# One slice of attention output work half a step later, function tables loaded in other stages, and a later first store

## The chip, the cores and the metric

The kernel runs on one core of one Trainium2 chip. The time is that of one whole launch, from inputs in the chip's main memory to outputs there, in device microseconds (us). Lower is better. PE is the tensor engine (matmuls; its weight loads overlap them), DVE the vector engine, ACT the scalar engine, POOL the general engine, SP the engine whose queue issues most transfers. Every engine works its own list of instructions in the order in which the program was written, and waits on semaphores for the others.

## The reference

A two-layer encoder trunk on one sequence of 256 tokens, width 1024, float32. Layer 0 mixes tokens by latent attention (MLA), layer 1 by forgetting attention (FoX). Around each mixer stand two half-step feed-forward blocks, and a gated per-layer embedding (PLE) ends the layer.

```python
for i in range(DEPTH):
    h = h + 0.5 * swiglu(rms_norm(h, ffn_norm[i, 0]), ffn_w_in[i, 0], ffn_w_out[i, 0])
    u = rms_norm(h, mix_norm[i])
    if i % N_MIXERS == 0:
        h = h + mla_mixer(u, cos, sin, ...)      # 8 heads, ends in o @ w_o
    else:
        h = h + fox_mixer(u, ...)                # 8 heads, ends in o @ w_o
    h = h + 0.5 * swiglu(rms_norm(h, ffn_norm[i, 1]), ffn_w_in[i, 1], ffn_w_out[i, 1])
    gate = jax.nn.sigmoid(rms_norm(h, ple_norm[i]) @ ple_w_gate[i])
    h = h + gate * (p[i] @ ple_w_proj[i])
return rms_norm(h, final_norm)
```

## The kernel before

The residual `state` stays on the chip, transposed: 8 blocks of 128 features by 256 tokens. All weights stream in once, as a list of 128x1024 tiles (`plan`). Class `Weights` brings each through three steps: SP issues the transfer into `raw`, ACT rounds it to `whi` (L98), DVE subtracts to get the rest, `wlo` (L102). PE then multiplies activations by both parts (L228 with `whi`, 512 columns; L229 with `wlo`, 256 columns). `W.pump()` prepares one tile; `W.catch_up()` does so only when fewer than a given number of tiles are ready ahead of the one in use. Where the calls stand in the program sets where these instructions stand in ACT's and DVE's lists.

The feed-forward stage `ffn` ends in a loop over 8 output blocks `d`: PE fills `po`, DVE adds it to `state` (L384), ACT and DVE write the next stage's input `u` and its square.

Both mixers end in `attention`. Its loop over `h` (a "step" below) is a pipeline of heads. In step h, DVE scales the probabilities of head h-2 (`shares`, tile `pr`), PE transposes those of head h-lag (`turn`, tile `pt`, copied to `ptS` by ACT), PE makes the scores of head h-1 (`scores`, tile `psc`; then maximum on DVE, `nm`, exponential on ACT at L425 and L426), and PE multiplies by the values of head h-lag (`values`, tile `po`), which ACT (L208) and DVE (L209) split into `os`. The lag is 3 in MLA, 2 in FoX. In MLA's steps 0 to 5 PE also projects queries; from step 6 on it has only this chain and the output projection w_o.

`fill_some(n)` hands PE n pairs of w_o matmuls (L228, L229), each pair one head of one output block (tile `ps`, named `ps2` in the source), taking only heads below `ready`. A step has two places for it: place 0 before `turn`, place 1 behind `scores` and ahead of `values`. `MLA_FILLS` and `FOX_FILLS` say how many at (step, place).

`ple_by_token` ends the kernel: per half of the tokens (t) and per column half or quarter, PE computes a gate, `gated` runs sigmoid (ACT L810), multiply and add (DVE L811, L812), square with a sum (ACT L813) and a gain multiply (DVE L814). `store(t)` turns the sums into a factor (DVE L820, L821, POOL L822), scales two halves (ACT L823, DVE L824) and issues two output transfers (L826).

ACT needs the right function table before an exponential, sigmoid, sine, logarithm or silu; the compiler puts an ACT_TABLE_LOAD ahead of the first that needs another one. `ready[P, 1]` with `AF.Silu` at L190 loads the first table while inputs are on their way.

Of the kernel before, what the change touches and what calls it, by code (L numbers as in the profile page):

```python
# [11 lines left out]
F32 = mybir.dt.float32  # L12
# [3 lines left out]
AF = mybir.ActivationFunctionType  # L16
ALU = mybir.AluOpType
# [23 lines left out]
GAINS = 80  # L41


MLA_FILLS = {(6, 0): 3, (7, 0): 3, (8, 0): 3, (8, 1): 4, (9, 0): 4, (9, 1): 4, (10, 1): 3}
FOX_FILLS = {(8, 0): 4, (8, 1): 7, (9, 0): 6, (9, 1): 5}

PI_IN = 3.1415925
# [94 lines left out]
def trunk(ctx, tc, xT, xt, pT, pos, freq, bf, ffn_first, ffn_in, ffn_out, w_down, w_uq, w_ukv, mla_o,  # L142
# [42 lines left out]
    state = const.tile([P, GAINS + KD * T], F32, name="state")  # L185
    g_sb, hT = state[:, :GAINS], state[:, GAINS:].rearrange("p (k t) -> p k t", k=KD)

    ready = const.tile([P, 1], F32, name="ready")
    nc.vector.memset(ready, 0.0)
    nc.scalar.activation(ready, ready, AF.Silu)  # L190
    ident = const.tile([P, P], F32, name="ident")
    make_identity(nc, ident)
    ones = const.tile([P, P], F32, name="ones")
# [117 lines left out]
            self.rb2 = self.rb.rearrange("p (o t) -> p o t", o=1).to_broadcast([P, 2, T])  # L311


    def ffn(norm, nxt, first=None, meanwhile=None, later=None):
        hs = big.tile([P, KF, 2, T], F32R, name="hs", tag="big")
        meanwhile = meanwhile or iter(())
        gu, hid = {}, {}

        def evacuate(c, i, ps):
            two = work.tile([P, 2, T], F32, name="two", tag="pair2", bufs=4)  # L320
            nc.vector.tensor_mul(two, ps, norm.rb2)  # L321
            gu[c, i] = tmp("gu")
            nc.gpsimd.tensor_add(gu[c, i], two[:, 0, :], two[:, 1, :])  # L323

        def hidden(c):
            h = hid.pop(c)
            split(hs[:, c, 0, :], hs[:, c, 1, :], h)

        def gate(c, ps, pumps=1):
            evacuate(c, 0, ps)  # L330
            W.pump(pumps)
            if c:
                hidden(c - 1)
            sg = tmp("sg")
            nc.scalar.activation(sg, gu.pop((c, 0)), AF.Silu)  # L335
            gu[c, 0] = sg

        def up(c, ps, pumps=1):
            evacuate(c, 1, ps)
            hid[c] = tmp("hid")  # L340
            nc.gpsimd.tensor_mul(hid[c], gu.pop((c, 0)), gu.pop((c, 1)))  # L341
            W.pump(pumps)
            if c % 2:
                W.catch_up()

        waits = [(bank("pg"), bank("pu"))]
        if first:
            waits.append((bank("pg"), bank("pu")))
            first([p for ps in waits for p in ps])
        else:  # L350
            blocks(waits[0], norm.pair)
            W.pump(2)
        at = len(waits)
        for c in range(at, KF):
            pg = bank("pg")
            block(pg, norm.pair)
            if c == at:
                norm.by_token()
                W.pump()
            else:  # L360
                gate(c, pg)
            pu = bank("pu")
            block(pu, norm.pair)
            if c == at:
                norm.by_column()
                for x, ps in enumerate(waits):
                    gate(x, ps[0], x)
                    up(x, ps[1], 0)
                gate(c, pg)
            up(c, pu, c > at)  # L370
        for d in range(KD):
            ps = bank("po")
            for a in range(0, KF, KD):
                w, = W.get()
                part(ps, w, hs, range(a, min(a + KD, KF)), KF - 1, at=lambda k: (k - a) * P)
                W.done(w)
                if a + KD < KF:
                    W.pump()
                    if d == a == 0:
                        hidden(KF - 1)  # L380
                    for _ in range(2):
                        next(meanwhile, None)
            for i in range(2):
                nc.vector.scalar_tensor_tensor(hT[:, d, :], ps[:, i, :], 0.5, hT[:, d, :], op0=ALU.mult, op1=ALU.add)  # L384
            if d < KD - 1:
                nxt.high(d, hT[:, d, :])
                W.pump()
                nxt.low(d, hT[:, d, :])
                nxt.square(hT[:, d, :])
            else:  # L390
                nxt.last(d, hT[:, d, :])
                W.pump()
            W.catch_up()
            for _ in range(2):
                next(meanwhile, None)
            if later:
                later(d)
        for _ in meanwhile:
            pass


    def attention(project, score, v, scale, nxt, lag, fills, early, cumq=None):
# [92 lines left out]
        for h in range(H + lag):  # L495
            if 0 <= h - 2 < H:
                shares(h - 2)
            if h == H:
                W.pump()
            if h < H and not late:  # L500
                project(h, 0)
            fill_some(fills.get((h, 0), 0))
            if 0 <= h - lag:
                turn(h - lag)
            if h < H and late:
                project(h, 0)
            if 0 <= h - 1 < H:
                scores(h - 1)
            if h < H:
                project(h, 1)  # L510
            W.catch_up()
            fill_some(fills.get((h, 1), 0))
            if 0 <= h - lag:
                values(h - lag)
            if h >= H:
                W.catch_up()
            ready = h - lag + 1
        for n in (H - 1, H):
            for d in range(early):
                fill(d, n)  # L520
# [115 lines left out]
    def fox(norm, nxt):  # L636
# [11 lines left out]
        def gates():  # L648
# [10 lines left out]
            nc.vector.tensor_scalar(u, e, 1.0, None, op0=ALU.add)  # L659
            nc.vector.scalar_tensor_tensor(e, u, 1.0, e, op0=ALU.subtract, op1=ALU.subtract)  # L660
            nc.scalar.activation(u, u, AF.Ln)
            yield
            nc.vector.tensor_sub(u, u, e)
            nc.vector.scalar_tensor_tensor(z, z, 0.0, u, op0=ALU.min, op1=ALU.subtract)
# [89 lines left out]
    def ple(pp, norm, nxt):  # L754
# [20 lines left out]
        for c in range(2):  # L775
            w, = W.get()
            for i in range(4):
                if i % 2 == 0:
                    pe = bank("pe")
                if (c, i) == (1, 3):  # L780
                    norm.by_column()
                part(pe[:, i % 2, :], w, pp, range(2), at=lambda k: k * 512 + i * P)
                if i % 2:
                    nc.scalar.activation(es[:, 4 * c + i - 1:4 * c + i + 1, :], pe, AF.Copy)
            W.done(w)
            if c == 0:
                norm.by_token()
            W.pump(2)
        for d in range(KD):
            ps = bank("ps", (P, T))  # L790
            block(ps, norm.pair)
# [2 lines left out]
    def ple_by_token(pp, norm):  # L794
# [21 lines left out]
        def store(t, n):  # L816
# [3 lines left out]
            nc.vector.reduce_sum(s, sums[:, t, :n], axis=AX.X)  # L820
            nc.vector.tensor_scalar(v, s, 1.0 / D, EPS, op0=ALU.mult, op1=ALU.add)  # L821
            nc.gpsimd.tensor_tensor(r, v, mhalf[:, :1], op=ALU.pow)  # L822
            nc.scalar.activation(h[:, t, half[0]], es[:, t, half[0]], AF.Copy, scale=r)  # L823
            nc.vector.tensor_scalar(h[:, t, half[1]], es[:, t, half[1]], r, None, op0=ALU.mult)  # L824
            for e, a in zip((nc.scalar, nc.sync), half):
                e.dma_start(out[t * P:(t + 1) * P, a], h[:, t, a])  # L826


        for c in range(2):
# [32 lines left out]
        for t in range(2):  # L862

            cuts = [half[1]] if t == 0 else [slice(N, N + N // 2), slice(N + N // 2, D)]
            for i, a in enumerate(cuts):
# [2 lines left out]
                    b = (k % 2 - 1) * N  # L868
                    rows(last, ws[k // 2], norm.pair, k, slice(a.start + b, a.stop + b), t, KD - 1)
                gated(t, last, a, 1 + i)  # L870
            store(t, 1 + len(cuts))
        W.done(*ws)


# [159 lines left out]
                yield  # L1034

    n1 = Norm(G_MIX, KD, D)
    ffn(n0, n1, first, tables())
    for i in range(2):
        n2 = Norm(G_FFN + 8 * (2 * i + 1), KD, D)
        if i == 0:  # L1040
# [2 lines left out]
            fox(n1, n2)  # L1043
        n3 = Norm(G_PLE + 8 * i, KD, D)
        p = Embedding(i)
        ffn(n2, n3, later=p)
        if i == 0:
            n0, n1 = Norm(G_FFN + 16, KD, D), Norm(G_MIX + 8, KD, D)
            ple(p.pair, n3, n0)
            ffn(n0, n1)  # L1050
        else:
            ple_by_token(p.pair, n3)

# [89 lines left out]
```

## Time and profile before

| | |
|---|---|
| time, median of 3 runs | 1018.78 us (1017.39 to 1019.54) |
| time of the profiled execution | 1017.48 us |
| its span, first to last instruction | 1015.4 us |
| PE busy | 993.2 us, 98% |
| DVE busy | 741.9 us, 73% |
| ACT busy | 517.2 us, 51% |
| POOL busy | 424.7 us, 42% |
| granted PE clock, mean | 0.994 of full speed |

The profiled execution took 2.1 us beside its span. A share of busy time is a mean over stages, so the rows further down look at single stages: who is idle, and for whom it waits.

### The profile page before, as it was taken

The page shows a single profiled execution, that of the slowest core. Times are in us where ns is not written, and L with a number is a line of the kernel's source. Part 1 is how long each engine was busy: PE and PEld are TensorE (multiplying, and loading weights), DVE is VectorE, ACT ScalarE, POOL GpSimd, SP SyncE. Part 2 cuts the span into 40 slices and gives each one's busy share as a digit, 9 for nine tenths or more (in the row PEclk, how much of TensorE's full clock was granted, in tenths as well). Part 3 has the DMA queues.
Part 4 walks back from the last instruction along what each step waited for, and adds up shares of the span by engine and source line. Part 5 has one row for each costly group of instructions (what it writes and reads, how often), then busy time and mean ns, then how long its engine had stood idle before and what let it go on. Part 6 is the DMA issues. An engine that isn't in the chain of part 4 may idle for free.

```text
span 1015.4 us, 16002 instructions
## 1 busy us (share of the span) xinstructions
PE 993.2 (98%) x5940; PEld 877.1 (86%) x5940; DVE 741.9 (73%) x1050; ACT 517.2 (51%) x821; POOL 424.7 (42%) x348
## 2 busy tenths in 40 slices
PE   9999999997999999999999999999999999999996
PEld 7888888986888888889888888889888888888885
DVE  5777878674677888667877887666776778876674
ACT  7555544464455545446555544456544555444553
POOL 0777720110157776111377774120221477672110
PEclk9999999998999999999999999999999999999999
DMA  9567666541257656665457666655542566666561
GB/s 325 174 208 209 196 177 194 185 146 45 79 173 210 200 187 177 202 192 187 132 188 210 197 187 178 201 183 170 183 146 85 186 207 194 191 184 205 174 205 42
DMA packets 51388, 180.54 MB, mean 178 GB/s; under 512 B 5872, under 2 KB 6000, under 8 KB 51312
## 3 DMA queue, kind: packets, MB, share of 16 engines
q1 hardware_dynamic: 50736, 178.49, 56.5%
q8 instruction: 47, 0.77, 0.3%
q10 hardware_dynamic: 576, 1.05, 0.3%
q14 instruction: 29, 0.24, 0.1%
HBM read 178.46 MB, written 1.05 MB: 177 GB/s over the span
## 4 chain that ended last, share of the span: by engine, by line
PE 92%; DVE 4%; ACT 2%; issue 1%; DMA 1%; SPq 0%; POOLq 0%; POOL 0%; ACTq 0%
PE po L228 16%; PE pu L228 16%; PE pg L228 16%; PE po L229 8%; PE pu L229 8%; PE pg L229 8%; PE ps L228 5%; PE ps L229 2%; PE ps L215 1%; PE ps L214 1%; PE ps L213 1%; DVE wlo L102 1%; PE pv L213 1%; PE pv L215 1%; PE pv L214 1%
## 5 line engine op out<-in xcount | busy, mean ns | idle before, releaser
L102 DVE TENSOR_TENSOR wlo<-raw,whi 128x1024 fp32r<-128x1024 f32 (+2 forms) x338 | 418.2, 1246 | 10.6 <-ACT whi L98 10.0
L98 ACT ACTIVATE whi<-raw 128x1024 fp32r<-128x1024 f32 (+2 forms) x338 | 335.9, 1027 | 21.7 <-DMA raw<-in_ffn_in_dram 12.5
L323 POOL TENSOR_TENSOR gu<-two 128x256 f32<-128x256 f32 x176 | 235.4, 1338 | 117.9 <-DVE two L321 108.5
L228 PE MATMUL pg<-u,whi 128*128 128x512 f32 x704 | 251.9, 395 | 2.4 <-DVE u L272 1.5
L228 PE MATMUL pu<-u,whi 128*128 128x512 f32 x704 | 251.2, 394 | 0.0
L228 PE MATMUL po<-hs,whi 128*128 128x512 f32 x704 | 246.3, 394 | 0.0
L229 PE MATMUL pg<-u,wlo 128*128 128x256 f32 x704 | 198.4, 282 | 0.5 <-DVE wlo L102 0.5
L229 PE MATMUL pu<-u,wlo 128*128 128x256 f32 x704 | 198.1, 281 | 0.0
L229 PE MATMUL po<-hs,wlo 128*128 128x256 f32 x704 | 198.1, 281 | 0.0
L228 PEld LDWEIGHTS pg<-u,whi 128*128 128x128 f32 x704 | 132.3, 188 | 33.8 <-DVE u L272 2.5
L228 PEld LDWEIGHTS po<-hs,whi 128*128 128x128 f32 x704 | 132.2, 188 | 30.4
L228 PEld LDWEIGHTS pu<-u,whi 128*128 128x128 f32 x704 | 132.3, 188 | 30.2
L229 PEld LDWEIGHTS pg<-u,wlo 128*128 128x128 f32 x704 | 132.5, 188 | 1.4 <-DVE wlo L102 1.4
L229 PEld LDWEIGHTS pu<-u,wlo 128*128 128x128 f32 x704 | 132.5, 188 | 0.0
L229 PEld LDWEIGHTS po<-hs,wlo 128*128 128x128 f32 x704 | 132.5, 188 | 0.0
L283 POOL TENSOR_TENSOR acc<-acc,sq 128x256 f32<-128x256 f32 x42 | 47.1, 1121 | 174.9 <-ACT sq L278 174.7
L208 ACT ACTIVATE hs<-hid 128x256 fp32r<-128x256 f32 x88 | 36.8, 419 | 142.4 <-POOL hid L341 140.3
L341 POOL TENSOR_TENSOR hid<-sg,gu 128x256 f32<-128x256 f32 x88 | 105.1, 1195 | 7.0 <-POOL gu L323 0.2
L209 DVE TENSOR_TENSOR hs<-hid,hs 128x256 fp32r<-128x256 f32 x88 | 63.5, 722 | 48.6 <-ACT hs L208 48.6
L267 ACT ACTIVATE u<-state 128x256 fp32r<-128x256 f32 x57 | 29.0, 508 | 130.8 <-DVE state L384 109.1
L321 DVE TENSOR_TENSOR two<-pg,rb 128x512 f32<-128x512 f32 x88 | 60.3, 686 | 47.3 <-PE pg L229 39.1
L335 ACT ACTIVATE sg<-gu 128x256 f32<-128x256 f32 x88 | 36.8, 418 | 78.6 <-POOL gu L323 78.6
(251 smaller groups left out, 1193.8 us busy)
## 6 DMA issues: line engine op xcount, KB each, us to landing
raw<-in_ffn_in_dram SPq DMA_DIRECT2D x172, 512.0 KB, 3.6
raw<-in_ffn_out_dram SPq DMA_DIRECT2D x64, 512.0 KB, 3.6
raw<-in_ffn_out_dram SPq DMA_DIRECT2D x32, 384.0 KB, 3.7
raw<-in_fox_qk_dram SPq DMA_DIRECT2D x16, 512.0 KB, 3.6
raw<-in_mla_o_dram SPq DMA_DIRECT2D x8, 512.0 KB, 3.4
raw<-in_ple_gate_dram SPq DMA_DIRECT2D x8, 512.0 KB, 4.9
raw<-in_fox_o_dram SPq DMA_DIRECT2D x8, 512.0 KB, 3.6
raw<-in_ple_rows_dram SPq DMA_DIRECT2D x8, 512.0 KB, 4.7
```

Of the source, the lines that this page charges most:

```text
L98: self.nc.scalar.activation(self.pairs[i][0][:, c], self.raws[i][:, c], AF.Copy)
L102: self.nc.vector.tensor_sub(lo[:, c], self.raws[i][:, c], hi[:, c].bitcast(F32))
L208: nc.scalar.activation(hi, src, AF.Copy)
L209: nc.vector.tensor_sub(lo, src, hi.bitcast(F32))
L228: nc.tensor.matmul(ps, hi, x[:, k], start=k == 0, stop=False)
L229: nc.tensor.matmul(ps[:, 1, :], lo, x[:, k, 0, :], start=False, stop=k == last)
L267: nc.scalar.activation(self.pair[:, b, 0, c], src[:, c], AF.Copy, scale=g)
L283: nc.gpsimd.tensor_add(new, self.acc, sq)
L321: nc.vector.tensor_mul(two, ps, norm.rb2)
L323: nc.gpsimd.tensor_add(gu[c, i], two[:, 0, :], two[:, 1, :])
L335: nc.scalar.activation(sg, gu.pop((c, 0)), AF.Silu)
L341: nc.gpsimd.tensor_mul(hid[c], gu.pop((c, 0)), gu.pop((c, 1)))
```

## The change

Five edits. The variable `ready` in `attention` is set ahead of place 1 of a step and lags: at place 0 of a step the newest head allowed is one older than before. MLA's three pairs at (6, 0) and (7, 0) go to place 1 of the same step; the other counts stay. A helper `table(f)` runs a one-element activation, which makes the compiler load f's table there; each `ffn` calls it at d = 1 for the function of the stage that follows, and FoX calls it behind its logarithm. In `ple` one `W.pump()` fewer stands in the opening loop. In `ple_by_token` the store of the first half of the tokens comes behind the third of the four last `gated` calls, both its halves are scaled on DVE, and both its transfers go by SP.

```diff
-MLA_FILLS = {(6, 0): 3, (7, 0): 3, (8, 0): 3, (8, 1): 4, (9, 0): 4, (9, 1): 4, (10, 1): 3}
+MLA_FILLS = {(6, 1): 3, (7, 1): 3, (8, 0): 3, (8, 1): 4, (9, 0): 4, (9, 1): 4, (10, 1): 3}
...
+    def table(f):
+        nc.scalar.activation(ready[:, 1:], ready[:, :1], f)
+    table(AF.Silu)
...
             W.catch_up()
+            if d == 1:
+                table(then)
...
             W.catch_up()
+            ready = h - lag
             fill_some(fills.get((h, 1), 0))
...
-            ready = h - lag + 1
...
             nc.scalar.activation(u, u, AF.Ln)
+            table(AF.Exp)
...
-            W.pump(2)
+            W.pump(2 - c)
...
-            nc.scalar.activation(h[:, t, half[0]], es[:, t, half[0]], AF.Copy, scale=r)
-            nc.vector.tensor_scalar(h[:, t, half[1]], es[:, t, half[1]], r, None, op0=ALU.mult)
-            for e, a in zip((nc.scalar, nc.sync), half):
-                e.dma_start(out[t * P:(t + 1) * P, a], h[:, t, a])
+            for i, a in enumerate(half):
+                if t and i == 0:
+                    nc.scalar.activation(h[:, t, a], es[:, t, a], AF.Copy, scale=r)
+                else:
+                    nc.vector.tensor_scalar(h[:, t, a], es[:, t, a], r, None, op0=ALU.mult)
+                (nc.scalar if t and i == 0 else nc.sync).dma_start(out[t * P:(t + 1) * P, a], h[:, t, a])
...
                 gated(t, last, a, 1 + i)
-            store(t, 1 + len(cuts))
+                if (t, i) == (1, 0):
+                    store(0, 2)
+        store(1, 3)
...
-    ffn(n0, n1, first, tables())
+    ffn(n0, n1, AF.Exp, first, tables())
...
-        ffn(n2, n3, later=p)
+        ffn(n2, n3, AF.Sigmoid, later=p)
...
-            ffn(n0, n1)
+            ffn(n0, n1, AF.Exp)
```

PE's list in MLA, from the values of head 2 (end of step 5) into step 6, before the change (`ps` with `os` is w_o, `pt` the transposes of head 3, `psc` the scores of head 5):

```order
L448 MATMUL po<-ptS,kqv 128x128
L228 MATMUL ps<-os,whi 128x512
L229 MATMUL ps<-os,wlo 128x256
L228 MATMUL ps<-os,whi 128x512
L229 MATMUL ps<-os,wlo 128x256
L228 MATMUL ps<-os,whi 128x512
L229 MATMUL ps<-os,wlo 128x256
L440 MATMUL pt<-ident,pr 128x128 x3
L628 MATMUL psc<-kqv 128x128
L628 MATMUL psc<-kqv 128x256
```

The same place of PE's list in the changed kernel, whose line numbers are higher:

```order
L455 MATMUL po<-ptS,kqv 128x128
L447 MATMUL pt<-ident,pr 128x128 x3
L635 MATMUL psc<-kqv 128x128
L635 MATMUL psc<-kqv 128x256
L536 LDWEIGHTS identb
L536 MATMUL psc<-cmask,identb 128x2x128
L638 MATMUL psc<-kr,kqv 128x128
L638 MATMUL psc<-kr,kqv 128x256
L233 MATMUL ps<-os,whi 128x512
L234 MATMUL ps<-os,wlo 128x256
L233 MATMUL ps<-os,whi 128x512
L234 MATMUL ps<-os,wlo 128x256
```

The three pairs now stand behind the transposes and the scores; the lists of ACT, DVE and POOL in this stretch are the same as before.

ACT's list of the first feed-forward stage, around the two sines of the position tables, in the changed kernel:

```order
L283 ACTIVATE sq<-state 128x256
L98 ACTIVATE whi<-raw 128x1024 x2
L1031 ACT_TABLE_LOAD
L1031 ACTIVATE cs<-st 128x256
L1032 ACTIVATE cs<-ang 128x256
L272 ACTIVATE u<-state 128x256
```

Before the change there is no load there (L1019 and L1020 follow `whi` directly). The exponential's table is loaded at d = 1 of this stage and the sines come behind it.

DVE's list at the end of the kernel, from the gain multiply of the third column half, in the changed kernel (L819, L820, L822 are `gated`; L828, L829, L835 are `store`):

```order
L822 TENSOR_TENSOR fin<-fin 128x512
L819 TENSOR_TENSOR sgr<-fin,sgr 128x256
L820 TENSOR_TENSOR fin<-fin,sgr 128x256
L822 TENSOR_TENSOR fin<-fin 128x256
L828 TENSOR_REDUCE s<-sums 128x1
L829 TENSOR_SCALAR v<-s 128x1
L835 TENSOR_SCALAR fin<-fin,r 128x512 x2
L819 TENSOR_TENSOR sgr<-fin,sgr 128x256
```

Before, the reduce, the scalar and one scaling stood ahead of the first 128x256 row.

## Rows read from the trace of the kernel before

**Rows 1.** Busy time by stretch: the stretch in us from the span's start, its length, then busy us and instructions of PE, of PE's weight loads, DVE, ACT and POOL, the granted PE clock, the share of the DMA engines, GB/s. Steps 0 to 5 of MLA's loop, parts of steps 6 to 10, and what follows.

```profile
217.00:235.00 18.00, 16.87 (x122) 15.13 (x121) 11.72 (x33) 10.84 (x28) 0.20 (x1) 1.00 0.37 117
...
239.27:242.68 3.41, 3.41 (x15) 2.86 (x14) 0.14 (x1) 0.49 (x1) 0.00 (x0) 0.50 0.20 82
...
246.10:249.51 3.41, 3.41 (x14) 2.85 (x13) 0.20 (x1) 0.49 (x1) 0.00 (x0) 0.50 0.00 0
249.51:265.00 15.49, 12.81 (x77) 10.88 (x76) 6.35 (x17) 5.64 (x15) 0.00 (x0) 1.00 0.23 69
265.00:293.00 28.00, 28.00 (x186) 25.46 (x185) 21.25 (x34) 16.75 (x27) 8.05 (x9) 1.00 0.48 150
```

**Rows 2.** Whom PE's matmuls waited for, over the whole span: us in total, times, longest.

```profile
PE ps L228 <- DVE os L209: 8.3, 5, 2.8
PE pg L228 <- DVE u L272: 1.5, 1, 1.5
PE pt L440 <- DVE pr L433: 1.1, 1, 1.1
...
PE pg L228 <- ACT whi L98: 0.8, 1, 0.8
```

**Rows 3.** PE in time order, MLA's steps 5 to 10: start us, us, engine, line, operation, tiles, shapes, count, and in brackets the idle time before it with what ended it.

```profile
235.03 0.48 PE L228 MATMUL ps<-os,whi 128*128 128x512 f32 x1
...
238.80 0.51 PE L228 MATMUL ps<-os,whi 128*128 128x512 f32 x1 [2.83 <-DVE os L209]
...
239.27 0.83 PE L440 MATMUL pt<-ident,pr 128*128 128x128 f32 x3
...
245.70 0.50 PE L228 MATMUL ps<-os,whi 128*128 128x512 f32 x1 [2.21 <-DVE os L209]
...
254.17 0.50 PE L228 MATMUL ps<-os,whi 128*128 128x512 f32 x1 [2.45 <-DVE os L209]
...
254.63 0.49 PE L440 MATMUL pt<-ident,pr 128*128 128x128 f32 x3
...
256.19 0.59 PE L228 MATMUL ps<-os,whi 128*128 128x512 f32 x1
...
256.74 0.40 PE L228 MATMUL ps<-os,whi 128*128 128x512 f32 x1
...
257.78 0.60 PE L447 MATMUL po<-ptS,kqv 128*128 128x256 f32 x2
...
258.36 0.48 PE L228 MATMUL ps<-os,whi 128*128 128x512 f32 x1
...
264.81 0.48 PE L228 MATMUL ps<-os,whi 128*128 128x512 f32 x1
```

**Rows 4.** ACT and DVE in the same form, steps 5 and 6: on ACT the split of head 2, the copy of head 3's transposes, the exponential of head 5 and the split of head 3; on DVE the scaling of head 4, the maximum of head 5 and the rest of the split of head 3.

```profile
237.91 0.38 ACT L208 ACTIVATE os<-po 128x256 fp32r<-128x256 f32 x1
...
240.19 0.49 ACT L442 ACTIVATE ptS<-pt 128x384 f32<-128x384 f32 x1 [1.90 <-PE pt L440]
...
243.82 0.46 ACT L425 ACTIVATE pr<-psc,nm,qscale 128x128 f32<-128x128 f32 x1 [3.13 <-DVE nm L416]
...
244.81 0.38 ACT L208 ACTIVATE os<-po 128x256 fp32r<-128x256 f32 x1
...
239.06 0.35 DVE L434 TENSOR_SCALAR pr<-pr,inv 128x256 f32<-128x256 f32 x1
...
242.88 0.29 DVE L412 TENSOR_REDUCE m<-psc 128x1 f32<-128x128 f32 x1 [3.47 <-PE psc L631]
...
245.22 0.42 DVE L209 TENSOR_TENSOR os<-po,os 128x256 fp32r<-128x256 f32 x1 [1.52 <-ACT os L208]
```

**Rows 5.** The table loads ahead of the exponential L425, one in each mixer, as a group over the span: operation, count, busy us and mean ns, idle time before them and whom it waited for.

```profile
L425 ACT ACT_TABLE_LOAD x2 | 2.6, 1283 | 5.3 <-DVE nm L416 2.7 <-DVE nm L422 2.6
```

**Rows 6.** DVE in the PLE stage of layer 0, block d = 3.

```profile
483.17 0.42 DVE L758 TENSOR_TENSOR zg<-ps,rb 128x256 f32<-128x256 f32 x1 [0.43 <-PE ps L215]
```

**Rows 7.** The end of the kernel, PE, ACT and DVE: the last matmul of t = 0's second half, the last of all, the sigmoid and the square of t = 0's second half, and on DVE the store's reduce and scaling and the multiply of the last quarter.

```profile
1000.63 0.39 PE L215 MATMUL ps<-wlo,u 128*128 128x512 f32 x1
...
1006.44 0.28 PE L215 MATMUL ps<-wlo,u 128*128 128x256 f32 x1
...
1001.07 0.68 ACT L810 ACTIVATE sgr<-ps,rtok 128x512 f32<-128x512 f32 x1
...
1003.23 0.63 ACT L813 ACTIVATE sgr<-fin 128x512 f32<-128x512 f32 x1 [1.49 <-DVE fin L812]
...
1003.99 0.15 DVE L820 TENSOR_REDUCE s<-sums 128x1 f32<-128x2 f32 x1
...
1004.99 0.49 DVE L824 TENSOR_SCALAR fin<-fin,r 128x512 f32<-128x512 f32 x1 [0.66 <-POOL r L822]
...
1006.65 0.43 DVE L811 TENSOR_TENSOR sgr<-fin,sgr 128x256 f32<-128x256 f32 x1 [1.18 <-ACT sgr L810]
...
1008.48 0.43 DVE L811 TENSOR_TENSOR sgr<-fin,sgr 128x256 f32<-128x256 f32 x1 [0.47 <-ACT sgr L810]
```

**Rows 8.** FoX's step 9: PE's one wait in w_o and its next transposes, and DVE's scaling of the probabilities that these read.

```profile
771.28 0.50 PE L228 MATMUL ps<-os,whi 128*128 128x512 f32 x1 [0.58 <-DVE os L209]
...
773.13 0.49 PE L440 MATMUL pt<-ident,pr 128*128 128x128 f32 x3
...
772.66 0.35 DVE L434 TENSOR_SCALAR pr<-pr,inv 128x256 f32<-128x256 f32 x1
```

More of the change, by code (lines that the diff above doesn't have):

```diff
@@ L186, in trunk @@
     g_sb, hT = state[:, :GAINS], state[:, GAINS:].rearrange("p (k t) -> p k t", k=KD)
-    ready = const.tile([P, 1], F32, name="ready")
+    ready = const.tile([P, 2], F32, name="ready")
     nc.vector.memset(ready, 0.0)
-    nc.scalar.activation(ready, ready, AF.Silu)
+    def table(f):
+        nc.scalar.activation(ready[:, 1:], ready[:, :1], f)
+    table(AF.Silu)
     ident = const.tile([P, P], F32, name="ident")
@@ L311, in by_column, with ffn @@
             self.rb2 = self.rb.rearrange("p (o t) -> p o t", o=1).to_broadcast([P, 2, T])
-    def ffn(norm, nxt, first=None, meanwhile=None, later=None):
+    def ffn(norm, nxt, then, first=None, meanwhile=None, later=None):
         hs = big.tile([P, KF, 2, T], F32R, name="hs", tag="big")
```

## The prediction

> **What bounds the kernel now.** PE is busy 98% of the span, so time can only come out of stretches in which PE waits or runs slowly, and out of the end, where PE has finished. I read the views in this order.
>
> First, whom PE waited for [rows 2]. Five waits of w_o on `os` make 8.3 us; the next input of a feed-forward stage is waited for once, 1.5 us; a transpose on scaled probabilities once, 1.1 us. A converted weight, `whi`, is waited for once in the whole span, 0.8 us. So the conversion of weights on ACT has slack nearly everywhere.
>
> Second, where those waits lie and at which clock [rows 1, 3]. Three of them, 2.83, 2.21 and 2.45 us, stand between 235 and 254 us, in MLA's steps 6 to 8. Behind the first and the second, PE runs 3.41 us each at half of full speed (1.2 instead of 2.4 GHz); the third and the 1.1 us wait, which lies in the stretch 217 to 235, are followed by full speed. What follows at 265 has PE busy for 28.00 of 28.00 us, so what MLA gives up earlier isn't lost again behind it.
>
> Third, why `os` is late there [rows 3, 4]. In step 6, PE's third w_o pair waits for head 2, whose split ACT begins at 237.91, behind the exponential of the step before. While PE waits, its next work (turn 3, scores 5) stands behind the wait, although the probabilities for it were ready. Hence DVE waits 3.47 us for scores 5, ACT's copy of the transposes waits 1.90, and the split of head 3 comes late for the next w_o pair. Each step pays the chain scores, maximum, exponential, split, w_o in series.
>
> **The change: w_o half a step later.** PE's list alone is permuted in this stretch; the number of matmuls, and the lists of ACT, DVE and POOL, stay. So I walk the new list with prices at full speed from the rows: turn and scores 1.56 us (254.63 to 256.19); four w_o pairs 1.59 (256.19 to 257.78), of which the last three take 1.04, so three pairs with a start 1.2 and two 0.85; values 0.58 (257.78 to 258.36) [rows 3]. Maximum to exponential 0.94, exponential to split 0.99, split to the first pair that may use it 0.89 (244.81 to 245.70), DVE's split to the end of the next scaled probabilities about 1.09 [rows 3, 4]; one `whi` between exponential and split 0.95, as the neighbouring steps have it (estimate).
>
> - Step 6 begins at 235.03. Turn and scores end 236.59, two pairs 237.44. Head 2's split isn't moved, since nothing ahead of it changed: PE waits until 238.80, now 1.36 us. Third pair 239.25, values 239.83.
> - DVE scales head 4 until 239.41 and finds scores 5 waiting: maximum at 239.41 instead of 242.88, exponential 240.35, split of head 3 at 241.34, usable 242.23.
> - Step 7: turn and scores end 241.39, a wait of 0.84, three pairs 243.43, values 244.01. Maximum 6 at 242.84, exponential 243.78, `whi`, split of head 4 at 245.72, usable 246.61.
> - Step 8: three pairs of older heads 245.21, turn and scores 246.77, four pairs 248.36, values 248.94; no wait. DVE's next `wlo` ends about 248.3, so split 5 is usable at 251.12.
> - Step 9: four pairs 250.53, turn (no scores left) 250.83, four pairs 252.42 (only the last needs head 5), values 253.00.
> - Step 10: turn 253.30, one pair 253.75, a wait of 0.2 for head 6, two pairs 254.75, values 255.3.
>
> The next pair then begins at 255.3 instead of 264.81 [rows 3]: 9.5 us less. As a cross-check, the waits fall from 7.7 to 2.4 us (5.3) and the half-speed stretches give back 2 x 3.41 / 2 = 3.4; the rest, 0.8, is starts of groups behind waits, each some 0.1 dearer. The bounds: 5.3, if the same amount of half speed stays, and 10.3, if the starts cost nothing more.
>
> In FoX the lag of `ready` moves a pair off head 6, for which PE waits 0.58 us. The transposes behind it begin at 773.13, 0.12 us after DVE's scaling of their input ends (772.66 + 0.35) [rows 8], so PE would reach them early and wait there: 0.1 us, between 0 and 0.58.
>
> **Function tables.** A load takes 1.28 us [rows 5]. The one ahead of MLA's first exponential, which leads to the 1.1 us wait, isn't removed: the exponential's table is loaded at d = 1 of the first feed-forward stage, and the sines come behind it in the same stage and need another, as the new order shows. So this stage has two loads more and MLA keeps its own: nothing. In FoX a load moves from the attention into the gates, and PE waited for neither. In PLE of layer 0 the first sigmoid comes earlier, but by block 3 DVE already waits 0.43 us for PE [rows 6], and from there on the chain is DVE's own, so the gain ends in that wait: nothing. At the end the load goes as well, but the third sigmoid begins at 1001.07, when PE has just ended its bank at 1001.02 [rows 7]: nothing. The new loads in the feed-forward stages cost ACT 1.28 + 0.2 us each, hidden by the slack of weights named above; without that cover they would cost PE up to four times 1.5 and one sine load, 7.2 us.
>
> The Trainium skill speaks against this edit: "ScalarE: Activation LUTs", section "Table sets: the hidden batching unit", wants activations grouped by set, and an exponential between silu and sine breaks up a group. By the page's price of about 2.66 us per switch the two loads added in the first stage would be 5.3 us of ACT's time, where the row gives 2.6 (an estimate from the page; no row here shows a longer switch).
>
> **One pump fewer in PLE.** One `wlo` of some 1.2 us moves from ahead of the first gate to block 2. There DVE has 0.43 us of idle time [rows 6] plus what the missing load gave it; by the same prices its block 2 ends within 0.1 us of PE's block 3. So +0.1, bounds 0 and +0.7.
>
> **The first store later.** Before, store(0) keeps DVE from 1003.99 and the last quarter's multiply begins at 1008.48 [rows 7]. Now the third-quarter gate goes first: the square of the second half ends 1003.86, sigmoid until 1004.4, multiply, add and gain multiply of 0.45 each until 1005.75, then the reduce, 1.00 us to the scaling (1003.99 to 1004.99), two scalings of 0.49 overlapping a little until 1007.6. PE is done at 1006.72, so the sigmoid of the last quarter is ready by 1007.3, and its multiply begins at 1007.6: 0.9 us earlier, and everything behind it, transfers included, with it. The two early transfers on SP leave before the last ones are due. Bounds: 0.5 and 1.2.
>
> **Sum.** -9.5 - 0.1 - 0.9 + 0.1 = -10.4 us. The profiled execution, 1017.48 (span 1015.4 and 2.1 beside it), becomes 1007.1; the median, 1.3 higher, 1008.4.
>
> **Rivals.**
> - Half speed stays. The new waits of 1.36 and 0.84 us are shorter than those that half speed followed, and 1.1 was followed by none; still, one or two stretches would take back 1.7 to 3.4 us: 1010.1 to 1011.8.
> - The wait only moves. If a transpose, a score or a value matmul found no free bank, since blocks 2 and 3 of w_o open half a step earlier and hold theirs, PE would stop there for about what it stopped at w_o. The chain of one step leaves 3 banks of 7, and 2 are in use at a time; I give this little. Then the half-speed stretches and the store would be the gain, 4.3 us: 1014.5.
> - The loads reach PE in the feed-forward stages: 10.4 less 7.2 is a gain of 3.2, 1015.6. Against it, one weight wait of 0.8 us in the span [rows 2]. Here the skill's rule on sets would count; the trace so far bears out only its row price.
> - The other side: half speed through the whole of steps 6 to 10. PE's 17.9 us of matmuls there (255.3 less 235.03 in the walk, less 2.4 of waits) would take 35.8, so the next pair begins at 270.8, 6.0 us later than before; with the store, 5.1 slower: 1023.9. It decides once more than 10.4 us of these matmuls run at half speed; before, two stretches of 3.41 us held 3.4 us of them [rows 1].
> - More than the walk: the median may hold more half speed than the profiled execution; then 1005.
>
> **How the numbers follow.** Likeliest 0.62 (own range 1006.4 to 1010), half speed stays 0.16, the wait moves 0.08, loads 0.05, more 0.06, the other side 0.03. Without the moved wait, the loads, the other side and a part of "more", 0.2 in all, the range is 1005.5 to 1012. About 0.2%, 2 us, is what a measurement tells from no change: faster than 1016.7 are all cases but the other side and a fifth of the loads and the moved wait, 0.94; same 0.03; slower 0.03.
>
> **What would show it.** PE's waits on `os` near 2.5 us in all, the longest about 1.4; a granted clock of 1.00 from 217 to 265; the copy `ptS` of head 3 right behind the split of head 2; MLA's table load and its 1.1 us wait unchanged; twelve loads in place of ten; the first block of the next feed-forward stage some 9.5 us earlier, and the distance from there to the end shorter by about 1. Wrong would be: waits on `pt` or `po`, half speed behind a 1.4 us wait, or waits for `whi` or `wlo` behind d = 1.

## The result, and the profile after

| | before | after |
|---|---|---|
| time, median of 4 runs each, same chip | 1018.09 us (1016.94 to 1019.54) | 1007.03 us (1006.04 to 1008.03) |
| time of the profiled execution | 1017.48 us | 1006.36 us |
| its span | 1015.4 us | 1004.2 us |
| granted PE clock, mean | 0.994 | 0.998 |

The ratio is 0.9891, 95% interval 0.9872 to 0.9909: 11 us less. The prediction was 1008.4 us, range 1005.5 to 1012.0.

Where it went is read from the first matmul of each stage. These are the rows of PE's timeline, in the columns of [rows 3], at which a stage's sums of squares are multiplied (`pst`), FoX begins (`pz`) and the final stage begins (`ph`). Before the change:

```profile
213.05 0.54 PE L297 MATMUL pst<-ones,acc 128*128 128x1 f32 x4
...
287.66 0.50 PE L297 MATMUL pst<-ones,acc 128*128 128x1 f32 x4
...
467.66 0.50 PE L297 MATMUL pst<-ones,acc 128*128 128x1 f32 x4
...
504.89 0.28 PE L297 MATMUL pst<-ones,acc 128*128 128x1 f32 x2
...
982.49 0.71 PE L844 MATMUL ph<-ident,state 128*128 128x128 f32 x5
```

After:

```profile
212.62 0.54 PE L302 MATMUL pst<-ones,acc 128*128 128x1 f32 x4
...
277.50 0.50 PE L302 MATMUL pst<-ones,acc 128*128 128x1 f32 x4
...
457.50 0.50 PE L302 MATMUL pst<-ones,acc 128*128 128x1 f32 x4
...
494.92 0.50 PE L302 MATMUL pst<-ones,acc 128*128 128x1 f32 x4
...
972.36 1.91 PE L854 MATMUL ph<-ident,state 128*128 128x128 f32 x16
```

The differences of neighbours are the stages' lengths; the lengths of FoX come from the same rows at 696.55 and 799.39 before, 686.65 and 789.30 after:

| stage | before | after | difference | predicted |
|---|---|---|---|---|
| MLA's heads and w_o | 74.61 | 64.88 | -9.73 | -9.5 |
| feed-forward behind it | 180.00 | 180.00 | 0 | 0 |
| PLE of layer 0 | 37.23 | 37.42 | +0.19 | +0.1 |
| FoX | 102.84 | 102.65 | -0.19 | -0.1 |
| `ph` to the end | 32.91 | 31.84 | -1.07 | -0.9 |

The remaining 0.4 us lies in the first 10 us, where the programs are still the same: ACT's third rounding of a weight (L98), which waits for its transfer, begins at 8.18 us after the change and at 8.62 before. So that input landed 0.4 us earlier in this execution, and the whole rest of the first feed-forward stage keeps that lead.

Whom PE waited for after, as in [rows 2]: the 8.3 us on `os` have become 1.6, and three waits are left of five.

```profile
PE pg L233 <- DVE u L277: 1.8, 1, 1.8
PE ps L233 <- DVE os L214: 1.6, 3, 1.1
PE pt L447 <- DVE pr L440: 1.6, 2, 1.1
```

Stretches of MLA after, in the columns of [rows 1]: steps 6 to 10 now end near 255, at a clock of 1.00 throughout, and what follows has PE busy for all of its 27.70 us.

```profile
235.00:255.30 20.30, 18.68 (x113) 15.79 (x112) 10.49 (x31) 10.27 (x29) 0.00 (x0) 1.00 0.26 79
255.30:283.00 27.70, 27.70 (x185) 25.21 (x184) 21.40 (x34) 16.52 (x26) 8.22 (x9) 1.00 0.49 151
```

PE in time order after, to be held against [rows 3]. The transposes stand ahead of the wait, and the three waits on `os` are 1.06, 0.30 and 0.26 us:

```profile
234.70 0.49 PE L447 MATMUL pt<-ident,pr 128*128 128x128 f32 x3
...
238.38 0.51 PE L233 MATMUL ps<-os,whi 128*128 128x512 f32 x1 [1.06 <-DVE os L214]
...
241.71 0.50 PE L233 MATMUL ps<-os,whi 128*128 128x512 f32 x1 [0.30 <-DVE os L214]
...
253.25 0.51 PE L233 MATMUL ps<-os,whi 128*128 128x512 f32 x1 [0.26 <-DVE os L214]
...
254.06 0.59 PE L454 MATMUL po<-ptS,kqv 128*128 128x256 f32 x2
```

ACT and DVE at the place of [rows 4]. ACT copies the transposes right behind the split of head 2 (237.75; it waited 1.90 us), DVE finds the scores of head 5 as soon as it has scaled head 4 (238.89; it waited 3.47), and the split of head 3 begins 3.33 us behind that of head 2, where it took 6.90:

```profile
237.49 0.38 ACT L213 ACTIVATE os<-po 128x256 fp32r<-128x256 f32 x1
237.75 0.49 ACT L449 ACTIVATE ptS<-pt 128x384 f32<-128x384 f32 x1
...
240.82 0.38 ACT L213 ACTIVATE os<-po 128x256 fp32r<-128x256 f32 x1
...
238.89 0.28 DVE L419 TENSOR_REDUCE m<-psc 128x1 f32<-128x128 f32 x1
```

### The profile page after: what moved, and what is told of

Same layout as the page of the kernel before. It is cut to its first block, busy times and chain, and to the rows that moved or that the text cites. A ratio compares the mean times of both kernels' runs of the same rounds, so it can differ in the third digit from the quotient of the medians.

```text
span 1004.2 us, 16012 instructions
## 1 busy us (share of the span) xinstructions
PE 990.4 (99%) x5940; PEld 874.8 (87%) x5940; DVE 740.1 (74%) x1051; ACT 519.5 (52%) x827; POOL 425.0 (42%) x348
## 4 chain that ended last, share of the span: by engine, by line
PE 93%; DVE 4%; ACT 2%; issue 1%; POOLq 0%; POOL 0%; ACTq 0%
PE pu L233 16%; PE po L233 16%; PE pg L233 16%; PE po L234 8%; PE pu L234 8%; PE pg L234 8%; PE ps L233 4%; PE ps L234 2%; PE ps L220 1%; PE ps L219 1%; PE ps L218 1%; DVE wlo L102 1%; PE pv L218 1%; PE pv L220 1%; PE pv L219 1%
## 5 line engine op out<-in xcount | busy, mean ns | idle before, releaser
L98 ACT ACTIVATE whi<-raw 128x1024 fp32r<-128x1024 f32 (+2 forms) x338 | 335.5, 1027 | 17.3 <-DMA raw<-in_ffn_in_dram 11.6
```

The lines of the kernel that those rows point to most:

```text
L98: self.nc.scalar.activation(self.pairs[i][0][:, c], self.raws[i][:, c], AF.Copy)
```

## The experiments

Each kernel was timed beside the kernel before on the same chip; a ratio is to that. "MLA" and "PLE" below are the stage lengths of the table, each from the one profiled execution of that kernel, between the same `pst` rows (us from the span's start in brackets):

| kernel | MLA | PLE of layer 0 |
|---|---|---|
| before | 74.61 (213.05 to 287.66) | 37.23 (467.66 to 504.89) |
| order_only | 64.83 (213.23 to 278.06) | 38.96 (458.06 to 497.02) |
| places_only | 66.84 (212.95 to 279.79) | 37.18 (459.79 to 496.97) |
| ages_only | 64.66 (212.96 to 277.62) | 37.76 (457.62 to 495.38) |
| pads | 72.97 (212.56 to 285.53) | 37.04 (465.52 to 502.56) |
| pads3 | 71.37 (214.06 to 285.43) | 37.24 (465.43 to 502.67) |
| after | 64.88 (212.62 to 277.50) | 37.42 (457.50 to 494.92) |
| no_order | 72.80 (214.67 to 287.47) | 37.38 (467.47 to 504.85) |
| late_table | 63.60 (212.52 to 276.12) | 37.38 (456.12 to 493.50) |
| many_loads | 64.90 (212.89 to 277.79) | 37.38 (457.79 to 495.17) |
| pump2 | 64.92 (214.69 to 279.61) | 36.70 (459.61 to 496.31) |
| best | 63.41 (212.66 to 276.07) | 36.72 (456.07 to 492.79) |
| best_cut | 63.18 (214.12 to 277.30) | 36.71 (457.30 to 494.01) |

### Which half of the attention edit: the place or the age of the head

All of the edit alone (`order_only`): before, with the two lines of `ready` and the new `MLA_FILLS`.

> The kernel before with the attention edit alone (ready lags half a step, the pairs of steps 6 and 7 at place 1). If the attention edit is what saves, the distance from the sum of squares of MLA's input to that of the next feed-forward stage (74.6 us before, 64.9 in the changed kernel) falls to 64.9 and the whole to about 1008.5, 9.9 us under the kernel before. If table loads or the pump carry part of it, that distance stays above 66.

Ratio 0.9925 (0.9908 to 0.9943), median 1009.28 us; MLA 64.83. The stage's gain belongs to this edit.

The new table of places alone (`places_only`), the heads as old as before:

```diff
-MLA_FILLS = {(6, 0): 3, (7, 0): 3, ...
+MLA_FILLS = {(6, 1): 3, (7, 1): 3, ...
```

> The kernel before with only the move of the pairs of steps 6 and 7 from place 0 to place 1; ready as before. By the walk, steps 6 and 7 run as in the changed kernel, and in step 8 the third pair at place 0 still waits for head 4, 1.7 us, which pushes turn, scores and all behind them: MLA stage 66.7 us, about 8 us under the kernel before. If the place alone were the cause: 64.9. If the age of the head alone were the cause: still near 74.

Ratio 0.9949 (0.9928 to 0.9969); MLA 66.84, at full clock. PE's waits on `os`, one of them new, for head 4 at place 0 of step 8:

```profile
238.71 0.50 PE L228 MATMUL ps<-os,whi 128*128 128x512 f32 x1 [1.07 <-DVE os L209]
...
246.29 0.50 PE L228 MATMUL ps<-os,whi 128*128 128x512 f32 x1 [1.59 <-DVE os L209]
```

The lag alone (`ages_only`), the pairs still at place 0, ahead of the transposes:

```diff
             W.catch_up()
+            ready = h - lag
             fill_some(fills.get((h, 1), 0))
...
-            ready = h - lag + 1
```

> The kernel before with only the lag of ready; the pairs of steps 6 and 7 stay at place 0, ahead of turn and scores, but take older heads. By the walk, step 6 spends 1.2 us on three pairs that wait for nothing, scores 5 still end before DVE is free for them at 239.4, and PE's wait moves to the values of head 3, about 0.9 us; the three pairs are paid early, so steps 8 to 10 begin 1.1 us sooner than in the changed kernel: MLA stage 64.0 us, about 10.6 under the kernel before. If the place ahead of turn and scores is what costs, this stays above 68.

Ratio 0.9919 (0.9900 to 0.9937); MLA 64.66, 0.7 us more than expected and 0.2 less than with the whole edit. PE's waits have moved to the copied transposes, in front of `values`; with 0.25 us left on `os` they come to 1.4 us in MLA, where places_only has 3.2:

```profile
238.63 0.70 PE L447 MATMUL po<-ptS,kqv 128*128 128x256 f32 x2 [0.64 <-ACT ptS L442]
...
242.90 0.70 PE L447 MATMUL po<-ptS,kqv 128*128 128x256 f32 x2 [0.54 <-ACT ptS L442]
```

So the stall is cured either by moving the pair behind the work that others need, or by giving it a head that is ready; the age does it fully (-9.95 us of the stage), the place to four fifths (-7.8), and with the age right the place is worth nothing. This ranking rests on the stage lengths; the intervals of the three ratios overlap.

### Chain or clock: what half speed had cost

`pads` keeps the slow order and fills PE's first two waits with matmuls on zeros whose result nobody reads; the chain of scores, maximum, exponential and split stays as it was. `pads3` fills the third wait as well (`h in (6, 7, 8)`).

```diff
+            if late and h in (6, 7):
+                pad = psm.tile([P, T], F32, name="pad", tag="small")
+                for _ in range(18 if h == 6 else 16):
+                    nc.tensor.matmul(pad, warm[:, :P], warm, start=True, stop=True)
             fill_some(fills.get((h, 0), 0))
```

> The kernel before with 18 and 16 bf16 matmuls on zeros (256 columns, about 0.107 us each, into a spare bank, not used by anything) ahead of the pairs at place 0 of steps 6 and 7, so that PE is busy where it waited; they add no result. If the half-speed stretches behind those waits cost 3.4 us, PE's granted clock is 1.00 through the stage, the waits on os shrink by what the padding takes, and the MLA stage falls from 74.6 to about 71.2 us. If half speed costs nothing here since other engines set the pace, it stays at 74.6; if the padding is in the way, it grows by up to 3.6.

> The kernel before with padding (matmuls on zeros that add no result) ahead of the pairs at place 0 of steps 6, 7 and 8. With two of the waits padded, one half-speed stretch was left, behind the third, and the MLA stage was 72.97 us against 74.61. If each stretch costs 1.7 us, now none is left and the stage is about 71.2; the waits themselves, some 6 us of chain, stay in it. If half speed isn't the cause of that gain, it stays near 73.

pads: ratio 0.9981 (0.9968 to 0.9995), MLA 72.97. The expected 71.2 was missed. The two slow stretches are gone, but the third wait, 2.46 us and not filled, is now followed by one:

```profile
235.00:250.69 15.69, 11.94 (x82) 9.94 (x80) 6.99 (x22) 6.98 (x19) 0.00 (x0) 1.00 0.17 47
250.69:254.10 3.41, 3.41 (x15) 2.86 (x14) 1.47 (x3) 0.49 (x1) 0.00 (x0) 0.50 0.50 132
```

pads3: ratio 0.9973 (0.9959 to 0.9987), MLA 71.37, with full clock from 235 to 265:

```profile
235.00:265.00 30.00, 27.75 (x182) 23.64 (x182) 13.03 (x37) 10.71 (x29) 0.00 (x0) 1.00 0.17 53
```

PE still waits 0.84 and 0.45 us for `os` behind the padding in pads, and 0.85, 0.45 and 0.70 in pads3, so the padding itself held nothing up. Of MLA's 9.7 us, half speed was 74.61 less 71.37 = 3.2, and the chain 71.37 less 64.88 = 6.5.

`no_order` is the changed kernel with the attention edit undone.

> The changed kernel with the attention edit undone (old ready, old places); tables, pump and store as changed. If the rest of the change is worth what the sum says, the MLA stage is back at 74 to 75 us, the distance from the first transposes of the last stage to the end stays at 31.8 (32.9 before), and the whole is about 1 us under the kernel before. If the table loads carry more, 2 us or more under it.

Ratio 0.9988 (0.9971 to 1.0005); MLA 72.80, PLE 37.38, `ph` to the end 31.83. The store's microsecond is there in the trace without the attention edit, but the ratio alone doesn't tell this kernel from the one before. (The store's three parts, its place, the scaling on DVE and the queue, weren't tried singly.) MLA is 1.8 us shorter than in the profiled execution of before, with the same order of the same matmuls, because one slow stretch followed its waits and not two; PE waited 8.3 us for `os` as before, and the first wait was followed by full speed:

```profile
235.00:245.90 10.90, 5.87 (x35) 4.78 (x34) 5.99 (x19) 4.61 (x14) 0.00 (x0) 1.00 0.13 48
245.90:249.31 3.41, 3.41 (x13) 2.90 (x13) 0.36 (x2) 0.49 (x1) 0.00 (x0) 0.50 0.00 0
```

### The function tables

`late_table` is the changed kernel with the exponential's table loaded at d = 6 of the first feed-forward stage, behind the sines. `many_loads` loads tables six times instead of once in each such stage, alternating between two functions.

```diff
-            if d == 1:
+            if d == (6 if first else 1):
                 table(then)
```

```diff
             if d == 1:
-                table(then)
+                for _ in range(3):
+                    table(AF.Silu if then != AF.Silu else AF.Exp)
+                    table(then)
```

> The changed kernel with the exponential's table of the first feed-forward stage loaded at d = 6, behind the sines, instead of d = 1. If the sines are what evicts it, there are ten loads instead of twelve, none ahead of MLA's first exponential, PE's 1.1 us wait on pr in step 1 to 3 is gone, and the MLA stage falls from 64.9 to about 63.8. If the wait has another cause (the maximum, the scores), it stays.

> The changed kernel with six activations of one element at d = 1 of every feed-forward stage instead of one, which alternate between silu's and the next stage's table: five loads where there was one, some 6 us more of ACT's time in each of the four stages. If the weights' lead covers ACT there, the distances over the feed-forward stages (180.0 and 179.86 us) stay within 0.2. If loads there reach PE, the whole is up to 4 x 6 = 24 us slower.

late_table: median 1005.09 us, ratio 0.9890 (0.9869 to 0.9912); MLA 63.60, 1.28 us less than after. The gain is read from the stage alone: the ratio is the change's own within its interval. The kernel has ten loads again. ACT at MLA's first exponential in the changed kernel:

```profile
219.89 1.28 ACT L432 ACT_TABLE_LOAD   x1 [2.69 <-DVE nm L423]
221.19 0.46 ACT L432 ACTIVATE pr<-psc,nm,qscale 128x128 f32<-128x128 f32 x1
```

And in late_table, where the load is gone from there and the longest wait on `pr` is 0.5 instead of 1.1 us:

```profile
219.81 0.46 ACT L432 ACTIVATE pr<-psc,nm,qscale 128x128 f32<-128x128 f32 x1 [2.71 <-DVE nm L423]
```

many_loads: ratio 0.9906 (0.9884 to 0.9929), and the three feed-forward stages behind the first are 180.00, 182.25 and 179.86 us long (after 180.00, 182.27 and 179.86). The first, from its `pb` matmuls (they spread the stage's factor `rtok`) to the next stage's `pst`, takes 189.13 us (23.76 to 212.89; after 189.15, 23.47 to 212.62). Each of the four has four more loads in it, sixteen in all. The group of loads (6 in the changed kernel), in the columns of [rows 5]:

```profile
L193 ACT ACT_TABLE_LOAD x22 | 28.2, 1283 | 1.1 <-PEq L1143 0.7
```

Loads in those stages cost nothing that these lengths show; the one in MLA costs its whole length.

### The pump in PLE

`pump2` is the changed kernel with `W.pump(2)` in place of `W.pump(2 - c)`.

> The changed kernel with the one pump of the layer-0 embedding stage put back, nothing else. The kernel best had this stage at 36.7 us against 37.4 in all kernels with one pump fewer. If the missing pump is the reason, this one has 36.7 too, and MLA's stage stays at 64.9; if it came from the other two differences of best, it stays at 37.4.

Median 1006.06 us, ratio 0.9888 (0.9872 to 0.9905); PLE 36.70 against 37.42 with the edit and 37.23 before. The pump edit costs +0.7: PLE takes 37.38 to 37.42 us in the four kernels with it and 36.70 to 36.72 in the three that have the early sigmoid table and both pumps. The early table is worth -0.5 against this execution of before; the stage of before isn't as steady, 37.04 to 37.76 us over five kernels (38.96 in a sixth, with a slow stretch), so the table's worth lies between -0.3 and -1.1. The ratio alone doesn't tell pump2 from the change. DVE and POOL around block 3 in pump2:

```profile
475.11 0.42 DVE L766 TENSOR_TENSOR zg<-ps,rb 128x256 f32<-128x256 f32 x1 [1.06 <-PE ps L220]
...
475.91 1.21 DVE L102 TENSOR_TENSOR wlo<-raw,whi 128x1024 fp32r<-128x1024 f32 x1
...
477.95 0.42 DVE L766 TENSOR_TENSOR zg<-ps,rb 128x256 f32<-128x256 f32 x1
...
474.98 0.73 POOL L288 TENSOR_TENSOR acc<-acc,sq 128x256 f32<-128x256 f32 x1 [2.13 <-ACT sq L283]
```

The same place in the changed kernel:

```profile
473.01 0.42 DVE L766 TENSOR_TENSOR zg<-ps,rb 128x256 f32<-128x256 f32 x1
...
473.93 1.77 DVE L102 TENSOR_TENSOR wlo<-raw,whi 128x1024 fp32r<-128x1024 f32 x1
...
476.42 0.42 DVE L766 TENSOR_TENSOR zg<-ps,rb 128x256 f32<-128x256 f32 x1
...
473.88 0.74 POOL L288 TENSOR_TENSOR acc<-acc,sq 128x256 f32<-128x256 f32 x1 [3.14 <-ACT sq L283]
```

Counted from the stage's start (459.61 and 457.50), block 3 begins at 15.50 and 15.51, the same; block 4 at 18.34 and 18.92. Between them stands one `wlo`, 1.21 us where POOL's add had ended and 1.77 where it had begun just ahead.

### A version with three parts set otherwise

`best` is the changed kernel with three parts of it set otherwise: the pairs at place 0 again with the lagging `ready`, the late table, and `W.pump(2)`. `best_cut` also splits the accumulation of the next stage's first blocks in three, so that PE would wait less for the last two inputs `u`:

```diff
-        for ks in (range(KD - 1), range(KD - 1, KD)):
+        for ks in (range(KD - 2), range(KD - 2, KD - 1), range(KD - 1, KD)):
```

> The changed kernel with three differences: the exponential's table of the first feed-forward stage behind the sines (d = 6), the pairs of steps 6 and 7 back at place 0 with ready still lagging, and both pumps of the layer-0 embedding stage back. From the stages measured: MLA 63.6 with the late table, 0.2 less with the older heads at place 0, so 63.4; the embedding stage, 37.4 us in kernels with one pump fewer and 37.0 to 37.8 in those without, 37.2; span 1002.5, about 1.5 us under the changed kernel. If the early table of the sigmoid needs the missing pump, the embedding stage is 37.4 or more.

> As best, with the first two products of a feed-forward stage cut in three (blocks 0 to 5 of both, block 6 of both, block 7 of both, instead of 0 to 6 and 7), so that PE has 2.1 us of work where it waits 1.7 us for the input's block 6 behind the embedding stage. Block 7 comes 2.2 us behind block 6 and then takes the wait over, so 0.5 us is gained in the embedding stage (36.7), no more; if the last block were in time, 1.7.

best: median 1004.30 us (1004.03 to 1004.56), ratio 0.9871 (0.9854 to 0.9887); MLA 63.41, PLE 36.72. Against the change that is 1.5 and 0.7 us by the stages and 2.2 by the spans (1002.0 and 1004.2); the intervals of the two ratios overlap. What PE still waits for in it:

```profile
PE po L454 <- ACT ptS L449: 1.2, 2, 0.6
...
PE pg L233 <- DVE u L277: 1.1, 1, 1.1
PE pt L447 <- DVE pr L440: 0.5, 1, 0.5
```

best_cut: median 1003.84 us, ratio 0.9868 (0.9853 to 0.9883). The wait on `u` falls from 1.1 to 0.6 us, and PLE stays at 36.71, where 0.5 us less was expected: the wait had cost the stage nothing that the cut gives back. The two kernels are not told apart.

## Why the prediction was right, and where its terms were off

- **The w_o walk, -9.5: right.** It put the waits at 1.36, 0.84 and 0.2 us; they were 1.06, 0.30 and 0.26. From the start of step 6 to the last values it took 19.72 us and the trace shows 19.36 (234.70 to 254.06). Of the 0.4 us, 0.2 stands already at DVE's first maximum in step 6 (238.89, where the walk, moved by the 0.33 us of its earlier start, has 239.08), and another 0.1 at that of step 7 (242.22 instead of 242.51); the `whi` between exponential and split stands where the walk put it, at its price. The split into 5.3 of waits, 3.4 of half speed and 0.8 of starts agrees with the measured 6.5 of chain (waits and starts) and 3.2 of half speed.
- **Half speed goes: right in this profile, not a constant.** None of the three shorter waits was followed by it, so neither this rival nor the one with half speed throughout came about. But the term was read from one execution, and no_order shows the slow order with one stretch, 1.8 us shorter; against such an execution the stage's gain would have been 7.9 (72.80 less 64.88). The prediction names this dependence on the execution of before only in its last rival; the bounds of its -9.5 leave it out.
- **The wait doesn't move to another matmul: right for this order.** No wait on a bank shows. In ages_only it does move, to `ptS`, at 0.6 us a time.
- **Tables, "nothing": right in four places, wrong in PLE.** MLA keeps its load and wait (219.89; `pt` 1.1 us), as said, and late_table prices what the early place forgoes at 1.28 us. In the feed-forward stages the cover holds for sixteen more loads. There are twelve loads instead of ten, as said. Loads out of their groups cost nothing in these stages, and putting the sines ahead of the exponential, which saves two loads, is worth 1.28 us, all of it in MLA. That is where the prediction weighed the rule of the Trainium skill, "ScalarE: Activation LUTs", section "Table sets: the hidden batching unit". The 2.66 us per switch that this page of the Trainium skill gives isn't seen: the exponential begins 1.30 us behind the start of its load (219.89 and 221.19), and without the load it begins 0.08 ahead of where the load began (219.81). At the end the third sigmoid waits for PE, as said:

```profile
990.93 0.69 ACT L818 ACTIVATE sgr<-ps,rtok 128x512 f32<-128x512 f32 x1 [1.17 <-PE ps L220]
```

- **PLE: two terms mis-sized that cancelled.** The tables' "nothing" was -0.5 against the profiled execution of before (-0.3 to -1.1 over the others), and the pump's +0.1 was +0.7, its upper bound. That the two nearly cancelled to +0.19 was luck. The step that failed is "from there on the chain is DVE's own, so the gain ends in that wait". The gain does end in block 3's wait (15.50 and 15.51 us, as before: 483.17 in [rows 6] less 467.66), but what DVE does behind it has no fixed price. The `wlo` costs 1.21 or 1.77 us, depending on whether POOL's add has begun. The early table moved the square, and so POOL's add, ahead of that `wlo`; the pump edit moved the two together again. In the kernel before this depends on the execution: the add had begun 0.24 us ahead of that `wlo` in the profiled one (1.77 us), but had ended ahead of it in pads and pads3 (1.21 us). The prediction had priced every `wlo` at 1.2.
- **The store, -0.9: right, -1.07.** DVE in the changed kernel, from the two scalings of the first store to the last quarter's multiply, in the form of [rows 7]:

```profile
996.54 0.88 DVE L835 TENSOR_SCALAR fin<-fin,r 128x512 f32<-128x512 f32 x2 [0.66 <-POOL r L830]
...
997.34 0.42 DVE L819 TENSOR_TENSOR sgr<-fin,sgr 128x256 f32<-128x256 f32 x1
```

  That multiply stands 24.98 us behind `ph`, and stood at 25.99 (1008.48 less 982.49). The prediction has 25.11 (1007.6 less 982.49): the chain reaches the two scalings 0.08 us sooner than it said, and they overlap by 0.05 more.
- **FoX, -0.1: -0.19.** The wait that the edit removes was 0.58, and most of it is met again in front of the transposes (0.47), as said. The gain comes with the attention edit: FoX takes 102.63 us in order_only and 102.82 in no_order.
- **The median.** The prediction added 1.3 us to the profiled execution because before's median stood so much above it. After, it stands 0.7 above. With 0.4 us of earlier inputs, which nobody could predict, and 0.4 of terms, that is the 1.4 us by which 1008.4 was too high.

One thing stays open: order_only and no_order, the two halves of the change, are by their ratios worth 7.6 and 1.2 us, which is 2.3 less than the change's 11.1, while the stages' lengths do add. The gap isn't clear of noise, since each of the three intervals reaches some 1.8 us to either side. The traces show two things that differ between executions and belong to no edit. In no_order PE waits at 24 us, in a part of the program that all kernels share, for a factor from POOL:

```profile
PE pb L312 <- POOL rtok L307: 1.5, 1, 1.5
```

Three more of the thirteen traces have this wait, pads3 (1.4), pump2 (1.7) and best_cut (1.4); order_only has 0.3 of it, the others none. In order_only's profiled execution PLE was 38.96 us, because half speed followed a wait there, of 2.03 us on `u`; whether that is what its other executions lost too can't be seen, since they have no trace.

```profile
489.48:492.89 3.41, 3.41 (x13) 2.93 (x12) 3.31 (x5) 2.38 (x4) 1.04 (x2) 0.50 0.00 0
```

## What to carry to other kernels

When PE is busy 98% of the time, look for a few places where a matmul that waits stands ahead of matmuls that other engines wait for: one such wait is paid again in every step of the pipeline. An operand one step older cured it wholly here, a later place alone to four fifths. A function table is free in a stage where ACT has slack and costs its full 1.28 us on a chain that PE waits for, so load it behind the last function of another set in the stage before. Price a short move by what will run beside it in the new place, not by the duration in the old one.

## What the runs showed of the hardware

- **Half speed behind a wait is not certain, and varies between executions.** In the profiled executions waits of 2.03 us (order_only), 2.46 (pads), 2.83 and 2.21 (before), 2.20 (no_order) were followed by 3.41 us at 1.2 GHz, while the third of before, 2.45 [rows 3], the first of no_order, 2.83, and one of 2.12 on `u` in ages_only were followed by full speed. In these thirteen traces the clock fell behind no wait of 1.8 us or less while PE had work left. A stretch costs 1.4 to 1.8 us (MLA takes 74.61 us with two in before, 72.80 and 72.97 with one in no_order and pads, 71.37 with none in pads3). Over 21 executions of the kernel before on one chip, the mean granted clock has steps: eleven at 0.996 with a median of 1015.4 us, five at 0.994 with 1017.6, four at 0.992 with 1019.7, one at 0.991 with 1022.3. A step of 0.002 is about what one such stretch takes from the mean (half of 3.41 in 1015 us). So much of the spread of the kernel before fits a varying number of slow stretches, which without traces of those executions isn't shown; the steps of time, 2.1 to 2.6 us, are longer than a stretch costs, so something else goes along with them, and the wait of 1.4 to 1.7 us on `rtok` is a second source of spread. The four executions of best, whose waits are short, lie within 0.5 us, those of best_cut within 1.6.
- **DVE and POOL take turns.** Besides the 1.77 us above, pump2 shows the reverse 4 us later: there DVE's `wlo` began first, took 1.22 us, and POOL's add began 0.02 behind it:

```profile
478.90 1.22 DVE L102 TENSOR_TENSOR wlo<-raw,whi 128x1024 fp32r<-128x1024 f32 x1
...
478.92 1.80 POOL L288 TENSOR_TENSOR acc<-acc,sq 128x256 f32<-128x256 f32 x1 [3.21 <-ACT sq L283]
```

  Whichever began first took its usual time, and the other some 0.6 to 1.1 us more. The Trainium skill says so in "SBUF — State Buffer", section "SBUF: two separate sides": a DVE operation with both inputs in that memory and a POOL operation that reads it share a pair of ports by an exclusive lock, held for the whole instruction. The rows agree. POOL's factor `rtok` at the start shows one half of it: it takes 0.71 us in before and 1.58 in pump2, where a `wlo` of DVE begins 0.21 us ahead of it; but a `wlo` that begins 0.31 us behind it, in before, takes its usual 1.23.
